# Attention gate columns computed by half products behind the heads, and applied from HBM

## The chip, the cores and the metric

One core of a Trainium2 chip runs the whole kernel. The metric is device time in microseconds; the kernel before takes 1495.14 us (median of 3 runs). TensorE (PE) multiplies, VectorE (DVE), ScalarE (ACT) and GpSimd (POOL) do the rest; transfers are issued from the queue of SyncE (SP), some from ACT's.

## The reference

```python
h = rms_norm(x, norm_w)                                  # x: 512 x 2048
(a_q, a_f, a_i, a_g, b_q, b_k, b_v, b_g, gate_a, gate_b) = split(h @ w_in)   # 8 x 1024, 2 x 2048 columns
ya = hgrn2_mixer(a_q, a_f, a_i, ...) * silu(a_g)
yb = diff_attention(b_q, b_k, b_v, ...) * silu(b_g)      # 8 heads of 128 columns
mixed = sigmoid(gate_a) * (ya @ w_branch_a) + sigmoid(gate_b) * (yb @ w_branch_b)
out = x + mixed @ w_out
```

The change concerns `b_g`, the 1024 gate columns of the attention, and `silu(b_g)`.

## The kernel before

All products are made from fp32r pieces: a factor is split into a rounded high part and a remainder, and a product of two factors is three matmuls (high-high, high-low, low-high). The stages follow each other on PE:

1. `proj_a` and `mix_a` (to about 465 us): the recurrent branch.
2. Eight attention heads. `proj_b(head)` (L445) projects `h` to 512 columns of the head: q, k, v and gate, 128 each. Its `gemm` (L164) walks 8 blocks of two K tiles; per block it loads 128x2x512 weights (L177), rounds them on ACT (L182), takes the remainder on DVE (L183), and issues 24 matmuls of 512 columns (L198), 192 in a head. `evac_rows` (L225) copies the four PSUM accumulators out on ACT (L228). Then q and k are normalised (L458 to L463) and the gate columns go through `silu` (L240).
3. `mix_b(head)` (L469) is the attention itself: eight transposes of q and k (L476), gains on ACT and DVE (L482, L483), six small copies between partition halves on ACT's DMA queue (L486 to L489), scores of four row blocks (L512, L513) through a minimum on DVE (L515) and an exponential on ACT (L518), the combination of the two softmaxes on DVE (L526), transposes of the weights (L534) and the values (L541). Block 0 to 2 are twelve score matmuls, block 3 is four. `finish` (L250) normalises the head's output, multiplies by the gate (L267), transposes it (L274, in `turn`, run later inside a following `gemm`), splits it and writes high and low part to `y_d` (L280).
4. Beside heads 3 to 6, `stage` (L718) prepares the half-sums of `h` for stage 6 (two of eight steps per head; each reads two 256 KB tiles of x and writes five to `hs_d`).
5. Four `gemm`s with `w_a`.
6. `halved` (L600): the two merge gates, 16 groups of 256 columns. A group is made by seven half products (a 2x2 scheme with seven multiplications instead of eight), each of 8 matmuls of 512 and 8 of 256 columns (L693). Per half product ACT rounds a quarter of the weights (L653), DVE takes the remainder (L654) and, for four, adds quarters (L645). `gate_dual` (L897) combines the results, applies the sigmoid (L899), in the first eight groups multiplies by `z_d` (L902), and writes `g_d`.
7. Four `gemm`s with `w_b` on `yb` read from `y_d`, and `halved` again for `w_out`.

The order on each engine is fixed when the program is built: a scheduler simulates a timeline and puts the instructions of different heads between each other, PE's matmuls of `mix_b(head)` among those of `proj_b(head + 1)`. At run time every engine keeps that order and waits where an operand isn't ready. Small tiles come from 49 slots handed out first in, first out (`Slots`, L48), so a new tile waits for the last reader of the tile that had its slot. PSUM has four accumulators for `gemm` and four `mix` tiles.

Of the kernel before, what the change touches and what calls it, by code (L numbers as in the profile page):

```python
# [17 lines left out]
P = 128  # L18
# [48 lines left out]
def hybrid_block(ctx: ExitStack, tc: tile.TileContext, xT, w_in, w_a, w_b, w_out,  # L67
# [96 lines left out]
    def gemm(wsrc, nk, a_hi, a_lo, stationary_w, evac, before=None, after=None, done=None, turn_at=1):  # L164
        accs = [acc_tile() for _ in range(4)]
        nb = nk // KC
        for kb in range(nb):
# [10 lines left out]
            with tc.high_priority(offset=PRIO):  # L178
                step = 1 if before is not None and kb == 0 else KC
                for c in range(0, KC, step):  # L180
                    cs = slice(c, c + step)
                    nc.scalar.activation(out=whi[:, cs, :], in_=raw[:, cs, :], func=AF.Copy)  # L182
                    nc.vector.tensor_tensor(out=wlo[:, cs, :], in0=raw[:, cs, :], in1=whi[:, cs, :].bitcast(F32),  # L183
                                            op=SUB)
# [3 lines left out]
            for j in range(4):  # L188
                for c in range(KC):
                    k = kb * KC + c  # L190
                    js = slice(j * P, (j + 1) * P)
                    if stationary_w:
                        prods = ((whi[:, c, js], a_hi[k]), (whi[:, c, js], a_lo[k]), (wlo[:, c, js], a_hi[k]))
                    else:
                        prods = ((a_hi[k][:, js], whi[:, c, :]), (a_hi[k][:, js], wlo[:, c, :]),
                                 (a_lo[k][:, js], whi[:, c, :]))
# [28 lines left out]
    def evac_rows(tiles):  # L225
        def evac(j, acc):
            s = slots.get()
            nc.scalar.activation(out=s[0], in_=acc, func=AF.Copy, scale=rstd_t[:, j:j + 1])  # L228
# [21 lines left out]
    def finish(o, gates, gain, rz, dest):  # L250
# [15 lines left out]
        for i in range(NT):  # L266
# [4 lines left out]
        def turn():  # L271
# [3 lines left out]
            slots.put(sq)  # L275
            yh, yl = slots.get(F32R), slots.get(F32R)
# [168 lines left out]
    def proj_b(head, done=None):  # L445
        tiles = []

        def src(raw, kb):
            rows = w_in[kb * KC * P:(kb + 1) * KC * P, 4 * WA:8 * WA].rearrange("(c p) (s n) -> p c s n", p=P, s=4)
            return [(raw[:, c, :].rearrange("p (s n) -> p s n", s=4), rows[:, c, :, head * P:(head + 1) * P])  # L450
                    for c in range(KC)]

        gemm(src, NK, h_hi, h_lo, False, evac_rows(tiles), turn_at=3 if head > 3 else 1, done=done)
# [12 lines left out]
        silu([s[0][:, 384:512] for s in tiles])  # L466
        return tiles

    def mix_b(head, tiles, bias, dest):  # L469
# [88 lines left out]
        finish(o, [t[0][:, 384:512] for t in tiles], gb, rz, dest)  # L558
# [181 lines left out]
    g_d = dram.tile([2, NK, P, T], F32, name="g_d")  # L740
    y_d = dram.tile([2, 2, NWA, P, T], F32, name="y_d")
# [104 lines left out]
    def freed_by(tiles, quarters, w, c0):  # L846
        def done(kb):
            raws2.extend((tiles[0][kb][1], tiles[1][kb][1]))
            if kb < 2:
                for name, half, c in (("11", 0, 0), ("12", 0, 1), ("22", 1, 1), ("21", 1, 0))[2 * kb:2 * kb + 2]:  # L850
                    quarters[name] = load_quarter(w, half, c0 + c * D // 2, raws2)
# [9 lines left out]
    for g in range(4):  # L861
# [6 lines left out]
        def along(kb):  # L868
# [10 lines left out]
            if g == 3:  # L879
                freed_by(ya, quarters, w_in, 8 * WA)(kb)  # L880
# [16 lines left out]
    def gate_dual(which, n):  # L897
        def gated(t, e):
            nc.scalar.activation(out=t[0], in_=t[0], func=AF.Sigmoid)  # L899
# [6 lines left out]
        def right(st):  # L906
            add_halves(st[2][0][:, rh], st[1][0])
            slots.put(st[1])
            gated(st[2], NS + n)
# [3 lines left out]
        def emit(p, acc, st):  # L913
# [11 lines left out]
            elif p == 3:  # L925
# [4 lines left out]
                if which == 0:  # L930
                    for e in (NS + n, n):
                        st_z[e] = t = slots.get()
                        nc.sync.dma_start(out=t[0], in_=z_d[e])
# [6 lines left out]
    items = []  # L940
# [168 lines left out]
```

## Time and profile before

| | us |
|---|---|
| runs | 1494.73, 1495.14, 1498.22 |
| profiled execution | 1496.41 |
| its span | 1494.3 |
| PE busy | 1483.4 |
| DVE, ACT, POOL busy | 1033.6, 720.9, 82.6 |

Spans and busy times are of the one profiled execution. A matmul's record is longer than its share of a stream of matmuls, since they overlap; what one costs in a stream is the distance from its start to the next start.

### The profile page before, as it was taken

The numbers are of one execution on the slowest core, as the hardware profiler recorded it, in microseconds if no ns is written. First come the engines' busy times: TensorE is split into PE (matmuls) and PEld (weight loads), VectorE is DVE, ScalarE is ACT, GpSimd is POOL, SyncE is SP. The second block draws the span as 40 slices with busy tenths as digits, with TensorE's granted clock in tenths as the row PEclk, the third lists the DMA queues.
The fourth block names the chain that finished last, engine by engine and source line by source line (L and its number), as shares of the span: only waits on it lengthen the run. The fifth ranks groups of instructions, "written<-read, shape, count | busy, mean of one in ns | idle before, by whom it ended". The sixth has DMA issues, their size and how long they took to land.

```text
span 1494.3 us, 21762 instructions
## 1 busy us (share of the span) xinstructions
PE 1483.4 (99%) x7956; PEld 1285.0 (86%) x7956; DVE 1033.6 (69%) x2005; ACT 720.9 (48%) x1092; POOL 82.6 (6%) x94
## 2 busy tenths in 40 slices
PE   9999999999999999999999999999999999999998
PEld 8888888888888888888888888888888888879998
DVE  7656666575585556666766555888888866798775
ACT  7632642544524545555555544555554544344332
POOL 1000000000001101101101100000000000000000
PEclk9999999999999999999999999999999999999999
DMA  7332322322323446465458787555444465575540
GB/s 250 99 99 80 103 86 85 109 75 85 113 72 121 118 128 198 125 185 168 149 169 275 245 274 242 154 168 155 142 135 141 130 216 191 189 226 157 154 119 32
DMA packets 270874, 222.83 MB, mean 149 GB/s; under 512 B 13040, under 2 KB 230768, under 8 KB 270768
## 3 DMA queue, kind: packets, MB, share of 16 engines
q1 hardware_dynamic: 266704, 214.88, 46.1%
q10 hardware_dynamic: 3984, 6.31, 1.6%
q8 instruction: 62, 1.02, 0.3%
q14 instruction: 44, 0.36, 0.1%
q0 software_dynamic: 80, 0.26, 0.1%
HBM read 179.46 MB, written 35.65 MB: 144 GB/s over the span
## 4 chain that ended last, share of the span: by engine, by line
PE 93%; DMA 3%; DVE 2%; ACT 1%; SPq 1%; issue 0%; DVEq 0%; ACTq 0%
PE acc L198 54%; PE acc L693 26%; PE mix L693 4%; PE mix L317 3%; PE mix L541 1%; DMA s<-in_xT_dram 1%; PE mix L512 1%; PE mix L513 1%; PE mix L534 1%; DMA hs_d<-s 1%; PE mix L402 0%; DMA b<-in_w_in_dram 0%; PE mix L274 0%; DVE s L578 0%; DMA b<-in_w_b_dram 0%; PE mix L476 0%
## 5 line engine op out<-in xcount | busy, mean ns | idle before, releaser
L198 PE MATMUL acc<-b,b 128*128 128x512 f32 x3840 | 912.0, 393 | 2.7 <-ACT b L182 2.6
L198 PEld LDWEIGHTS acc<-b,b 128*128 128x128 f32 x3840 | 713.2, 188 | 146.2 <-ACT b L182 3.2
L183 DVE TENSOR_TENSOR b<-b,b 128x1024 fp32r<-128x1024 f32 (+1 forms) x161 | 195.7, 1216 | 183.4 <-ACT b L182 168.8
L182 ACT ACTIVATE b<-b 128x1024 fp32r<-128x1024 f32 (+1 forms) x161 | 169.2, 1051 | 277.7 <-PE acc L198 218.0
L653 ACT ACTIVATE b<-b 128x1024 fp32r<-128x1024 f32 x168 | 178.0, 1061 | 249.1 <-PE acc L693 155.6
L693 PE MATMUL acc<-s,b 128*128 128x256 f32 (+1 forms) x1792 | 284.4, 314 | 2.1 <-ACT b L653 1.0
L693 PEld LDWEIGHTS acc<-s,b 128*128 128x128 f32 x1792 | 255.3, 191 | 24.9 <-ACT b L653 1.2
L654 DVE TENSOR_TENSOR b<-b,b 128x1024 fp32r<-128x1024 f32 x168 | 205.3, 1222 | 34.5 <-ACT b L653 33.7
L693 PE MATMUL acc<-b,b 128*128 128x256 f32 (+1 forms) x896 | 143.4, 314 | 0.0
L693 PEld LDWEIGHTS acc<-b,b 128*128 128x128 f32 x896 | 128.2, 191 | 10.8
L645 DVE TENSOR_TENSOR b<-b,b 128x1024 f32<-128x1024 f32 x96 | 117.3, 1222 | 1.1
L693 PE MATMUL mix<-s,b 128*128 128x256 f32 (+1 forms) x448 | 72.5, 314 | 1.8 <-DVE b L654 1.3
L693 PEld LDWEIGHTS mix<-s,b 128*128 128x128 f32 x448 | 64.3, 191 | 7.6 <-DVE b L654 1.5
L333 DVE COPY_PREDICATED s<-s,mix 128x128 f32<-128x128 uint8 (+3 forms) x176 | 52.0, 338 | 14.1 <-PE mix L317 13.0
L577 ACT ACTIVATE s<-s 128x256 fp32r<-128x256 f32 x96 | 37.1, 411 | 49.3 <-DVE s L974 23.0
L518 ACT ACTIVATE s<-s,mn 128x128 f32<-128x128 f32 (+3 forms) x64 | 35.5, 555 | 24.8 <-DVE mn L515 24.7
L317 PE MATMUL mix<-qm,s 128*128 128x192 f32 x256 | 46.8, 326 | 0.0
L317 PEld LDWEIGHTS mix<-qm,s 128*128 128x128 f32 x256 | 42.7, 190 | 1.6
L461 POOL TENSOR_TENSOR qr<-qs,mhalf 128x4 f32<-128x4 f32 x32 | 35.4, 1116 | 114.8 <-DVE qs L460 114.8
L578 DVE TENSOR_TENSOR s<-s,s 128x256 fp32r<-128x256 f32 x96 | 38.3, 421 | 3.8 <-ACT s L577 3.5
L515 DVE CUSTOM_DVE_ANT_0 s<-mix,bias 128x128 f32<-128x128 f32 (+3 forms) x64 | 28.9, 487 | 13.1 <-PE mix L513 12.8
L228 ACT ACTIVATE s<-acc,rstd_t 128x512 f32<-128x512 f32 x48 | 32.5, 678 | 10.5 <-PE mix L541 7.3
(159 smaller groups left out, 1091.8 us busy)
## 6 DMA issues: line engine op xcount, KB each, us to landing
b<-in_w_in_dram SPq DMA_DIRECT2D x240, 256.0 KB, 3.0
b<-in_w_in_dram SPq DMA_DIRECT2D x64, 512.0 KB, 4.1
b<-in_w_out_dram SPq DMA_DIRECT2D x32, 512.0 KB, 4.2
s<-in_xT_dram SPq DMA_DIRECT2D x46, 256.0 KB, 4.1
hs_d<-s SPq DMA_DIRECT2D x40, 256.0 KB, 3.8
y_d<-s SPq DMA_DIRECT2D x32, 256.0 KB, 2.8
b<-y_d SPq DMA_DIRECT2D x32, 256.0 KB, 4.4
b<-in_w_a_dram SPq DMA_DIRECT2D x32, 256.0 KB, 4.0
```

The lines of the kernel that those rows point to most:

```text
L182: nc.scalar.activation(out=whi[:, cs, :], in_=raw[:, cs, :], func=AF.Copy)
L183: nc.vector.tensor_tensor(out=wlo[:, cs, :], in0=raw[:, cs, :], in1=whi[:, cs, :].bitcast(F32), op=SUB)
L198: nc.tensor.matmul(accs[j], lhsT=l, rhs=r, start=(k == 0 and n == 0), stop=(k == nk - 1 and n == 2))
L317: nc.tensor.matmul(ps[:, i * 192:(i + 1) * 192], lhsT=kt[:, tt * P:(tt + 1) * P], rhs=qm[:, tt * 192:(tt + 1) * 192], start=True, stop=True)
L333: nc.vector.copy_predicated(out=ov[:, :, a:b], mask=kv[:, :, s0:s0 + b - a], data=dv[:, :, s0:s0 + b - a])
L518: nc.scalar.activation(out=pr[c][0][:, 0:n], in_=pr[c][0][:, 0:n], func=AF.Exp, scale=-1.0, bias=mn[:, e:e + 1], accum_out=z[:, e:e + 1])
L577: nc.scalar.activation(out=out[..., lh], in_=x, func=AF.Copy)
L578: tt(out=out[..., rh], in0=x, in1=out[..., lh].bitcast(F32), op=SUB)
L645: tt(out=r[x][0], in0=r[x][0], in1=r[y][0], op=ADD)
L653: nc.scalar.activation(out=xh[0], in_=x, func=AF.Copy)
L654: tt(out=xl[0], in0=x, in1=xh[0].bitcast(F32), op=SUB)
L693: nc.tensor.matmul(o, lhsT=l, rhs=r, start=(first and ks[0] == 0 and n == 0), stop=(ks[-1] == NS - 1 and n == len(prods) - 1), skip_group_ ...
```

## The change

`proj_b` projects to 384 columns instead of 512: the weights read, rounded and multiplied are q, k and v alone, and `silu` leaves the heads. `finish` of a head multiplies by the row factor alone, now on ACT instead of DVE, and writes the transposed, ungated output in one tile to `yf_d`. The gate columns become four more groups at the head of `halved` in stage 6 (16 to 20 groups); their `gate_dual` applies Silu, multiplies by the head's output read back from `yf_d`, splits the product and writes it to `y_d`. The eight steps of `stage` are handed to heads 2 to 7 as 1, 1, 2, 1, 1, 2 instead of two each to heads 3 to 6.

```diff
-    def gemm(wsrc, nk, a_hi, a_lo, stationary_w, evac, before=None, after=None, done=None, turn_at=1):
+    def gemm(wsrc, nk, a_hi, a_lo, stationary_w, evac, before=None, after=None, done=None, turn_at=1, width=T):
...
-                    nc.scalar.activation(out=whi[:, cs, :], in_=raw[:, cs, :], func=AF.Copy)
...
+                    ws = slice(0, width)
+                    nc.scalar.activation(out=whi[:, cs, ws], in_=raw[:, cs, ws], func=AF.Copy)
...
-                        nc.tensor.matmul(accs[j], lhsT=l, rhs=r, start=(k == 0 and n == 0),
+                        nc.tensor.matmul(accs[j][:, ws], lhsT=l, rhs=r, start=(k == 0 and n == 0),
...
-        for i in range(NT):
+        for i in range(NT) if gates is None else ():
+            nc.scalar.activation(out=y[:, i * P:(i + 1) * P], in_=o[:, i * P:(i + 1) * P], func=AF.Copy,
+                                 scale=rr[:, i:i + 1])
+        for i in range(NT) if gates is not None else ():
...
+            if gates is None:
+                y_t = slots.get()
+                nc.scalar.activation(out=y_t[0], in_=yt, func=AF.Copy, scale=gain)
+                nc.sync.dma_start(out=yf_d[dest[1]], in_=y_t[0])
+                slots.put(y_t)
+                return
...
-        gemm(src, NK, h_hi, h_lo, False, evac_rows(tiles), turn_at=3 if head > 3 else 1, done=done)
+        gemm(src, NK, h_hi, h_lo, False, evac_rows(tiles, 3 * P), turn_at=3 if head > 3 else 1, done=done,
+             width=3 * P)
...
-        silu([s[0][:, 384:512] for s in tiles])
...
-        finish(o, [t[0][:, 384:512] for t in tiles], gb, rz, dest)
+        finish(o, None, gb, rz, dest)
...
+    STAGE = {1: (0,), 2: (1,), 3: (2, 3), 4: (4,), 5: (5,), 6: (6, 7)}
...
-        staged = [(k, stage_in(k)) for k in (2 * head - 4, 2 * head - 3)] if 2 <= head < 6 else []
+        staged = [(k, stage_in(k)) for k in STAGE.get(head, ())]
...
+        other = n + (NWA // 2 if which == 2 else NS)
+
         def gated(t, e):
+            if which == 2:
+
+                nc.scalar.activation(out=t[0], in_=t[0], func=AF.Silu)
+                z = st_z[e]
+                tt(out=t[0], in0=t[0], in1=z[0], op=MUL)
+                zh, tl = z[0].bitcast(F32R), t[0].bitcast(F32R)
+                nc.scalar.activation(out=zh, in_=t[0], func=AF.Copy)
+                tt(out=tl, in0=t[0], in1=z[0], op=SUB)
+                nc.sync.dma_start(out=y_d[1, 0, e], in_=z[0])
+                nc.sync.dma_start(out=y_d[1, 1, e], in_=t[0])
+                slots.put(z, t)
+                return
...
-    items = []
+    items = [(w_in, 7 * WA + n * P, 7 * WA + T + n * P, three_slots, gate_dual(2, n)) for n in range(NWA // 2)]
```

The scheduler makes another order of all this. PE, the scores of head 3, before: they stand inside the product of head 4 (L198), which goes on behind them; 30 of its matmuls stand between the last score of blocks 0 to 2 (L513) and the first transpose of the weights (L534). `s` are slots, `acc` the accumulators.

```order
L512 MATMUL mix<-s_366_5497,s_362_5482 128x256
L513 MATMUL mix<-s_368_5499,s_362_5482 128x256
...
L534 MATMUL mix<-ident,s_369_5512 128x128
L534 MATMUL mix<-ident,s_371_5529 128x128 x2
L512 MATMUL mix<-s_365_5496,s_361_5481 128x512
```

PE, the same place now (L522, L523 are the scores, L544 the transposes, L199 the product):

```order
L199 MATMUL acc<-b_327_5875,b_16_125 128x384
L522 MATMUL mix<-s_346_5440,s_342_5425 128x256 x2
L523 MATMUL mix<-s_348_5442,s_342_5425 128x256 x2
...
L523 MATMUL mix<-s_349_5443,s_343_5426 128x384
L544 MATMUL mix<-ident,s_350_5456 128x128
L544 MATMUL mix<-ident,s_352_5473 128x128 x2
L522 MATMUL mix<-s_346_5440,s_342_5425 128x512
...
L523 MATMUL mix<-s_349_5443,s_343_5426 128x512
L199 MATMUL acc<-b_330_6141,b_1_110 128x384
```

The twelve scores, the transposes and the four scores of block 3 have moved to the border between the products of heads 4 and 5; the first L199 row above is the last matmul of head 4, the last row the first of head 5, and nothing of a product stands between. Head 5's scores stand in the same way at the border of heads 6 and 7; at the border of head 7 and the `w_a` product stand head 6's second transposes and block 3.

ACT at that border, before: the copies of the product out of PSUM (L228) stand behind the copies of transposed weights (L536).

```order
L518 ACTIVATE s_377_5573,z<-s_377_5573,mn 128x512
L518 ACTIVATE s_378_5574,z<-s_378_5574,mn 128x512
L182 ACTIVATE b_333_6285<-b_332_6284 128x1024
L577 ACTIVATE s_439_6175<-s_400_5697 128x256
L536 COPY s_379_5595<-mix 128x384
L228 ACTIVATE s_406_5950<-acc,rstd_t 128x512
```

ACT now (L528 exponentials, L587 staging, L229 the copies out of PSUM, L546 copies of transposed weights):

```order
L528 ACTIVATE s_354_5490,z<-s_354_5490,mn 128x384
L587 ACTIVATE s_373_5610<-s_379_5618 128x256
...
L587 ACTIVATE s_377_5614<-s_380_5619 128x256
L528 ACTIVATE s_351_5457,z<-s_351_5457,mn 128x128
L528 ACTIVATE s_353_5474,z<-s_353_5474,mn 128x256
L528 ACTIVATE s_355_5491,z<-s_355_5491,mn 128x384
L229 ACTIVATE s_384_5887<-acc,rstd_t 128x384
L546 COPY s_356_5510<-mix 128x128
```

The first copy out of PSUM of head 4's product now stands behind the exponentials of the second softmax of head 3's blocks 0 to 2, and its slot (number 17) is the one of a softmax tile, `s_353_5474`, which it may overwrite only when DVE has combined block 1.

## Rows read from the trace of the kernel before

**Rows 1.** Page, parts 1 and 2: busy time and share of each engine; granted clock.

```profile
PE 1483.4 (99%) x7956; PEld 1285.0 (86%) x7956; DVE 1033.6 (69%) x2005; ACT 720.9 (48%) x1092; POOL 82.6 (6%) x94
PEclk9999999999999999999999999999999999999999
```

**Rows 2.** Stretches: PE, PEld, DVE, ACT, POOL busy (instructions), clock, DMA share, GB/s.

```profile
700.00:750.00 50.00, 50.00 (x246) 42.01 (x245) 36.27 (x100) 29.72 (x60) 6.50 (x6) 1.00 0.55 168
1000.00:1050.00 50.00, 50.00 (x289) 44.01 (x288) 44.52 (x53) 25.73 (x34) 0.00 (x0) 1.00 0.55 167
1200.00:1250.00 50.00, 47.73 (x257) 41.17 (x257) 28.39 (x33) 20.40 (x26) 0.00 (x0) 1.00 0.68 212
1300.00:1350.00 50.00, 46.69 (x283) 41.19 (x282) 46.63 (x88) 21.86 (x37) 0.00 (x0) 1.00 0.70 221
```

**Rows 3.** Timeline of PE in head 2: start, us, line, operation, tiles, shape, count.

```profile
565.95 10.23 PE L198 MATMUL acc<-b,b 128*128 128x512 f32 x44
...
600.34 0.33 PE L512 MATMUL mix<-s,s 128*128 128x384 f32 x1
600.51 0.62 PE L198 MATMUL acc<-b,b 128*128 128x512 f32 x2
600.97 0.34 PE L513 MATMUL mix<-s,s 128*128 128x384 f32 x1
601.15 2.46 PE L198 MATMUL acc<-b,b 128*128 128x512 f32 x10
```

**Rows 4.** Timeline of PE in `halved`: groups of 16 matmuls, 8 of 512, 8 of 256 columns.

```profile
957.52 2.96 PE L693 MATMUL acc<-b,b 128*128 128x512 f32 x16
960.31 2.96 PE L693 MATMUL acc<-s,b 128*128 128x512 f32 x16
...
977.07 2.96 PE L693 MATMUL acc<-b,b 128*128 128x512 f32 x16
```

**Rows 5.** Timeline of PE around head 4's attention.

```profile
693.29 0.93 PE L476 MATMUL mix<-ident,s 128*128 128x128 f32 x7
693.98 8.91 PE L198 MATMUL acc<-b,b 128*128 128x512 f32 x38
...
709.10 0.28 PE L513 MATMUL mix<-s,s 128*128 128x256 f32 x1
709.22 7.45 PE L198 MATMUL acc<-b,b 128*128 128x512 f32 x32
716.50 0.49 PE L534 MATMUL mix<-ident,s 128*128 128x128 f32 x3
...
717.75 0.63 PE L198 MATMUL acc<-b,b 128*128 128x512 f32 x2
```

**Rows 6.** Timeline of ACT in the same stretch (ACTq is its queue).

```profile
694.39 0.67 ACT L482 ACTIVATE s<-mix,gq 64x512 fp32r<-64x512 f32 x1
...
700.16 0.47 ACTq L489 DMA_DIRECT2D s<-s  x1
...
705.37 0.60 ACT L518 ACTIVATE s<-s,mn 128x384 f32<-128x384 f32 x1
```

**Rows 7.** Timeline of DVE there: the combination of blocks 0, 1 and 2.

```profile
711.52 1.27 DVE L526 SCALAR_TENSOR_TENSOR s<-s,f,s 128x128 f32<-128x128 f32 x3
```

**Rows 8.** Line L489, all heads: from issue of the copy to its landing.

```profile
DMA to landing us min/median/max: 2.3/4.5/6.5
```

**Rows 9.** Groups of instructions by line: count | busy us, mean ns | idle before.

```profile
L182 ACT ACTIVATE b<-b 128x1024 fp32r<-128x1024 f32 x159 | 168.0, 1056 | 277.2 <-PE acc L198 218.0 <-issue 21.5 <-DMA b<-in_w_in_dram 7.9
L183 DVE TENSOR_TENSOR b<-b,b 128x1024 fp32r<-128x1024 f32 x159 | 194.4, 1223 | 183.0 <-ACT b L182 168.4 <-PE acc L198 12.1 <-DMA b<-in_w_in_dram 1.2
L902 DVE TENSOR_TENSOR s<-s,s 128x512 f32<-128x512 f32 x16 | 11.0, 688 | 0.5 <-ACT s L899 0.5
```

**Rows 10.** Timeline of PE at the start, and its longest pause later.

```profile
1.04 6.30 PE L109 MATMUL mix<-ones 128*128 128x128 f32 x28 [1.04 <-DVE mhalf L103]
...
1233.70 1.66 PE L198 MATMUL acc<-b,b 128*128 128x512 f32 x6 [2.27 <-ACT b L182]
```

More of the change, by code (lines that the diff above doesn't have):

```diff
@@ L181, in gemm @@
                     cs = slice(c, c + step)
-                    nc.scalar.activation(out=whi[:, cs, :], in_=raw[:, cs, :], func=AF.Copy)
-                    nc.vector.tensor_tensor(out=wlo[:, cs, :], in0=raw[:, cs, :], in1=whi[:, cs, :].bitcast(F32),
-                                            op=SUB)
+                    ws = slice(0, width)
+                    nc.scalar.activation(out=whi[:, cs, ws], in_=raw[:, cs, ws], func=AF.Copy)
+                    nc.vector.tensor_tensor(out=wlo[:, cs, ws], in0=raw[:, cs, ws],
+                                            in1=whi[:, cs, ws].bitcast(F32), op=SUB)
             if after is not None and kb == nb - 1:
@@ L222, in two_cols, with evac_rows @@
         return src
-    def evac_rows(tiles):
+    def evac_rows(tiles, width=T):
         def evac(j, acc):
             s = slots.get()
-            nc.scalar.activation(out=s[0], in_=acc, func=AF.Copy, scale=rstd_t[:, j:j + 1])
+            nc.scalar.activation(out=s[0][:, 0:width], in_=acc[:, 0:width], func=AF.Copy, scale=rstd_t[:, j:j + 1])
             tiles.append(s)
@@ L448, in src @@
         def src(raw, kb):
-            rows = w_in[kb * KC * P:(kb + 1) * KC * P, 4 * WA:8 * WA].rearrange("(c p) (s n) -> p c s n", p=P, s=4)
-            return [(raw[:, c, :].rearrange("p (s n) -> p s n", s=4), rows[:, c, :, head * P:(head + 1) * P])
+            rows = w_in[kb * KC * P:(kb + 1) * KC * P, 4 * WA:7 * WA].rearrange("(c p) (s n) -> p c s n", p=P, s=3)
+            return [(raw[:, c, 0:3 * P].rearrange("p (s n) -> p s n", s=3), rows[:, c, :, head * P:(head + 1) * P])
                     for c in range(KC)]
-        gemm(src, NK, h_hi, h_lo, False, evac_rows(tiles), turn_at=3 if head > 3 else 1, done=done)
+        gemm(src, NK, h_hi, h_lo, False, evac_rows(tiles, 3 * P), turn_at=3 if head > 3 else 1, done=done,
+             width=3 * P)
         for s in tiles:
@@ L740, in hybrid_block @@
     g_d = dram.tile([2, NK, P, T], F32, name="g_d")
+    yf_d = dram.tile([NWA, P, T], F32, name="yf_d")
     y_d = dram.tile([2, 2, NWA, P, T], F32, name="y_d")
@@ L844, in hybrid_block, with freed_by @@
     vs, raws2 = [], deque()
-    def freed_by(tiles, quarters, w, c0):
+    def freed_by(tiles, quarters, w, c0, right=D // 2):
         def done(kb):
@@ L850, in done @@
                 for name, half, c in (("11", 0, 0), ("12", 0, 1), ("22", 1, 1), ("21", 1, 0))[2 * kb:2 * kb + 2]:
-                    quarters[name] = load_quarter(w, half, c0 + c * D // 2, raws2)
+                    quarters[name] = load_quarter(w, half, c0 + c * right, raws2)
         return done
@@ L879, in along @@
             if g == 3:
-                freed_by(ya, quarters, w_in, 8 * WA)(kb)
+                freed_by(ya, quarters, w_in, 7 * WA, T)(kb)
         gemm(two_cols(w_a, g * H, D // 2 + g * H), NWA, each(ya[0]), each(ya[1]), True, keep_z, done=along,
@@ L908, in right @@
             slots.put(st[1])
-            gated(st[2], NS + n)
+            gated(st[2], other)
         st_z, seen = {}, set()
@@ L929, in emit @@
                     right(st)
-                if which == 0:
-                    for e in (NS + n, n):
+                if which != 1:
+                    for e in (other, n):
                         st_z[e] = t = slots.get()
-                        nc.sync.dma_start(out=t[0], in_=z_d[e])
+                        nc.sync.dma_start(out=t[0], in_=z_d[e] if which == 0 else yf_d[e])
             else:
```

4 lines of the change are left out of this document (2 added, 2 removed).

## The prediction

> **What bounds the kernel now.** I read the busy shares first: PE has 1483.4 of 1494.3 us, and the clock is at its upper level throughout [rows 1]. Then the stretches [rows 2]: beside the heads (700 to 750) and the half products (1000 to 1050) PE is busy for all 50 us, while DVE has 36.3 and 44.5 us, ACT 29.7 and 25.7. The only breaks stand at the change to `w_b` (47.73 of 50) and the start of `w_out` (46.69); the change touches neither. So the time is the sum of PE's matmuls, as long as each finds its operands when PE comes to it. What a matmul costs in that sum is its distance to the next start. A change pays if it shortens that sum without making PE wait, and both have to be worked out.
>
> **The matmuls.** Removed: 8 heads x 192 = 1536 matmuls shrink from 512 to 384 columns. A run of 44 of 512 columns took 10.23 us [rows 3]; the last stretches 0.39 us past its start (L512, L513 and L198 single records), so (10.23 - 0.39)/43 = 0.229 us each; the runs of 38 and 32 in head 4 give 0.230 and 0.228 [rows 5]. I take 0.228. A matmul of 384 columns occurs in the scores: from L512 at 600.34 to the next start at 600.51 are 0.17 us, from L513 at 600.97 to 601.15 are 0.18 [rows 3]. I take 0.1745, between them. Saved: 1536 x 0.0535 = 82 us; with 0.230 and 0.17 it is 92, with 0.228 and 0.18 it is 74, but the records are rounded to 0.01 us and 256 columns cost 0.12 us (below), so that 384 half way between 0.12 and 0.228 is 0.174: the ends worth keeping are 79 and 85.
>
> Added: four groups of seven half products of 16 matmuls. Such sixteens start every 2.79 us (960.31 to 977.07 is six of them, 16.76 us, [rows 4]); a group is 7 x 2.793 = 19.55 us, four are 78.2. The arithmetic of seven instead of eight products would have saved more, but each half product is made of more and shorter matmuls: 8 of 512 take 8 x 0.228 = 1.82 us, so the 8 of 256 take 0.97, 0.12 each, more than half of 0.228. PE's sum: -82 + 78 = **-4 us**, between -7 and -1.
>
> The Trainium skill (TensorE: Matmul & The Clock Gate, "Back-to-back issue gap") puts a warm matmul of N columns at N/2.4 + 2.5 ns. By that page 1536 x 53.3 ns = 82 us go and 4 x 56 x (215.8 + 109.2) ns = 73 us come, so its sum would be -9 us. The rows disagree on the fixed part (0.12 us for 256 columns), and the measurement decides.
>
> **What hides the rest.** ACT and DVE lose more than they gain in the heads: 64 rounding and 64 remainder passes shrink by a quarter (DVE 1.22 us each, [rows 9], so about 0.3 us x 8 = 2.4 us a head), the silu goes. They were not the bound there, so this is worth nothing by itself. In the new groups DVE does two more subtractions than in the first merge groups (L902's kind, 0.69 us, [rows 9]): 44.5 us in 50 [rows 2] is 17.4 in 19.55; with 1.4 more it is 18.8, 96%. The rounding runs some half products ahead, so I take 0; if DVE needed all the idle time that it has now (2.15 us a group), it costs 1.4 x 4 = 5.5 us. The 8 writes and 8 reads of `yf_d` and the 16 writes of `y_d` go through SP among loads; DMA is at 0.55 in the gate stretch [rows 2] and the `w_b` product that needs `y_d` comes sixteen groups later: 0. Staging: two steps move from heads 3 to 6 into heads 2 and 7 (per step two reads and five writes of 256 KB on SP, ahead of the following weight loads). With two steps a head PE never paused in 700 to 750 [rows 2]: 0, and up to 2 us at head 7, where `ya` is loaded too.
>
> **The new wait.** A head's product now takes 192 x 0.1745 = 33.5 us instead of 43.8, but the attention that runs beside it is a chain with the same length. In the order above this shows at the border of heads 4 and 5: all sixteen scores of head 3 and the transposes that need their softmax stand back to back, with no matmul of a product between them. Behind them in PE's queue is the whole product of head 5, and it couldn't pass anyway: its accumulator is freed by L229, which waits for DVE's combination of block 1. Everything after waits with it. What PE pays there, in us after head 3's last transpose of q and k (L486):
>
> - PE has 36 matmuls of head 4 left: 36 x 0.1745 = 6.3.
> - The second softmax needs the third pair of copies to the other partition half. In head 4 of the kernel before the last transpose ended at 693.29 + 0.93 = 694.22 and the last copy (L489) was issued at 700.16, 5.9 later [rows 5, 6]. Now a rounding stands ahead of that copy on ACT and waits for head 4's last matmuls: 6.3 and three quarters of 1.06 [rows 9], 7.1.
> - Landing: 4.5 (2.3 to 6.5, [rows 8]), so 11.6.
> - Six matmuls with the low part of k, 0.5; minimum, exponential and combination up to block 1: in head 4 from the last L513 at 709.10 to the end of the second combination, about 712.3, 3.2 [rows 5, 7]; now the exponentials of three blocks (0.60 for 384 columns, [rows 6]) and four staging copies stand ahead, up to 4.1. I take 3.6: 15.7.
> - Transposes of blocks 0 and 1 and the scores of block 3: 716.50 to 717.75 = 1.25 [rows 5]. Head 5 starts at 17.0.
>
> Of these 17.0 PE worked 6.3 + 1.7 (twelve scores, 8 x 0.12 + 4 x 0.175) + 1.25 = 9.25. The pause is 7.7 us; with the short ends (5.9, 2.3, 3.2) it is 4.0, with the long ones (7.1, 6.5, 4.1) 10.2. The other end of the pause would be none if something of a product stood between, and nothing does. At the border of heads 6 and 7 the same order stands behind 38 matmuls (6.6 us), with three more staging copies ahead of the copy: 3.7 to 11.3, middle 7.5. I take 7 for each, below the middle, since with PE and the DMA queues idle the copies land sooner. At the border of head 7 and `w_a` the softmax has been given 33 + 6 matmuls (6.8 us) against 3.2 to 4.1 needed; the first `w_a` matmul waits for one L229 behind a rounding and a staging copy: about 0.6 us (0 to 2). At the other borders the products start with no score run ahead: 0.
>
> **Sum.** -4 + 7 + 7 + 0.6 = +10.6 us on a span of 1494.3, so about 1505; the profiled execution (1496.41) is 1.3 us over the median 1495.14, so against the median 1495.1 + 10.6 = 1505.7, rounded to **1506**.
>
> **Rivals.**
> - *The borders cost nothing* (not slower): the softmax chain is done when PE gets there, because ACT and DVE have less to do in a head. Then -4: 1491. For it: PE has not paused in any head, whatever the order. Against it: in head 4 the chain from the last transpose to the combination of block 1 took 712.3 - 694.2 = 18 us [rows 5, 7], and now it has 6.3 + 1.7. It decides if that chain can be done in 8 us; two pauses below 2 us each would do.
> - *The clock falls in the pauses.* Rows show no pause over 2.27 us between matmuls [rows 10], and there the clock stayed up [rows 1]. At the start 28 matmuls of 128 columns took 6.30 us, 0.22 each, against (0.93 - 0.27)/6 = 0.11 in head 4 [rows 5, 10]: half the pace, the lower level, after PE had done nothing. If PE comes back at that pace for as long (6 us) after each of the two pauses, it loses 3 us each time: 1506 + 6 = 1512. The Trainium skill (TensorE: Matmul & The Clock Gate, Part 1) says that the gate halves the clock after idle time, which speaks against making PE wait here. The scores within the pause, a few matmuls, speak against the fall.
> - *DVE bounds the new groups*: 1506 + 5.5 = 1511.
>
> **Chances.** Pauses as worked out, total 3 to 18 us above the PE sum: 0.65. No pauses: 0.17. Clock falls as well: 0.12. DVE bounds the groups: 0.06. About 0.3% (4.5 us) is what a measurement of this kernel can tell from no change. Faster by more (below 1490.7) is a little over half of the second case: 0.10. Within it: the rest of that case, 0.07, and the pauses at their short ends (-4 + 8 = +4), 0.13: 0.20. Slower: 0.70. The range leaves out the no-pause cases below 1494 and the worst sums: 1494 (two pauses of 1.5 us) to 1515 (two of 11 us, or clock and middle pauses).
>
> **What would show it.** In the trace of the changed kernel: starts of L199 in the heads 0.174 us apart and sixteens of L703 2.79 us apart (PE's sum); pauses of PE ahead of L523 and L544 at the borders of heads 4 and 5 and of 6 and 7, ended by the copy's landing (L499) and by DVE's combination (L536), with no others in the heads; PE near 100% in the four new groups; the clock at 1.00 around the pauses. The prediction is wrong if those borders are closed up, if PE pauses in the new groups behind DVE, or if pauses stand where I have put none, at head 7 behind SP's queue above all.

## The result, and the profile after

The changed kernel takes 1510.99 us (median; 1510.54 to 1512.74) against 1495.65 for the kernel before on the same chip: ratio 1.0104, 95% interval 1.0092 to 1.0115, so 15.5 us or 1.0% slower. The forecast was 1506 within 1494 to 1515. The profiled execution took 1512.74 us with a span of 1511.0, 16.7 more than the span before; it is the slowest of the four, so the losses read from its trace are 1 to 2 us larger than those of the medians.

The page after, busy time and granted clock (parts 1 and 2), which answer to [rows 1]:

```profile
PE 1486.0 (98%) x8404; PEld 1337.0 (88%) x8404; DVE 1068.3 (71%) x2021; ACT 727.4 (48%) x1135; POOL 84.3 (6%) x94
PEclk9999999999999999899999999999999999999999
```

PE's busy time hardly moved, as the sum of the matmuls said, though it holds matmuls at the lower clock: slice 17 of the clock (604 to 642 us) is an 8 where [rows 1] has only nines. The stretches, with the columns of [rows 2]:

```profile
550.00:600.00 50.00, 50.00 (x309) 49.65 (x308) 28.94 (x83) 27.32 (x63) 6.92 (x6) 1.00 0.49 153
600.00:650.00 50.00, 45.12 (x260) 43.65 (x259) 32.02 (x92) 27.20 (x64) 7.90 (x7) 0.90 0.42 132
700.00:750.00 50.00, 44.12 (x258) 42.43 (x257) 32.46 (x96) 28.03 (x65) 6.77 (x6) 0.93 0.71 216
750.00:800.00 50.00, 46.85 (x234) 39.31 (x233) 25.27 (x77) 23.18 (x48) 7.59 (x6) 1.00 0.75 245
800.00:850.00 50.00, 48.40 (x233) 40.19 (x232) 21.85 (x70) 22.02 (x43) 1.01 (x1) 1.00 0.83 274
860.85:939.03 78.18, 78.18 (x449) 68.83 (x448) 70.58 (x82) 45.39 (x59) 0.00 (x0) 1.00 0.59 185
```

PE is full in the first heads and in the four new groups (the last row). It idles 4.9 and 5.9 us in the two stretches that hold the borders of heads 4/5 and 6/7, there with a mean clock of 0.90 and 0.93, and 3.2 and 1.6 us around head 7 and in `w_a`.

How long each stage lasted, from its first matmul to that of the next, in the profiled execution of every kernel of this study (us; "heads, w_a" is the sum of the three columns before it):

| kernel | heads 0-3 | heads 4-7 | w_a | heads, w_a | merge gates | w_b to the end |
|---|---|---|---|---|---|---|
| before | 209.0 | 203.6 | 97.7 | 510.3 | 312.5 | 260.6 |
| after | 164.0 | 185.2 | 101.2 | 450.4 | 389.4 | 260.7 |
| e1, staging back | 167.1 | 178.7 | 99.6 | 445.4 | 389.7 | 260.5 |
| e2, heads only | 168.5 | 190.1 | 102.2 | 460.8 | 311.9 | 260.6 |
| e3, groups only | 211.0 | 210.3 | 95.1 | 516.4 | 389.5 | 260.7 |
| e4, turn late | 168.4 | 164.3 | 96.8 | 429.5 | 389.4 | 260.5 |
| e5, before with turn late | 210.2 | 207.3 | 95.1 | 512.6 | 311.1 | 260.4 |
| e6, own slots | 164.4 | 159.6 | 128.8 | 452.8 | 389.3 | 260.5 |
| e7, pauses filled | 164.1 | 192.4 | 98.9 | 455.4 | 389.7 | 261.2 |
| e9, turn late, staging back | 165.9 | 165.9 | 97.2 | 429.0 | 389.9 | 260.8 |
| e10, before, new staging | 210.7 | 203.2 | 95.9 | 509.8 | 311.3 | 260.8 |
| e11, half the filling | 164.1 | 181.4 | 99.9 | 445.4 | 389.5 | 260.4 |

The groups cost 389.4 - 312.5 = 76.9 us in every kernel that has them. Heads and `w_a` gave back 59.9 us where the matmuls alone are worth 81. The missing 21 us are the loss.

**The pauses.** PE after, at the border of heads 4 and 5 (the place of [rows 5]; L278 is the turn, L486 the transposes of q and k, L522 and L523 the scores, L544 the transposes of the weights, L199 the product):

```profile
606.72 0.27 PE L278 MATMUL mix<-ident,s 128*128 128x128 f32 x1
606.83 0.27 PE L486 MATMUL mix<-ident,s 128*128 128x128 f32 x1
...
607.38 0.82 PE L486 MATMUL mix<-ident,s 128*128 128x128 f32 x6
607.95 6.50 PE L199 MATMUL acc<-b,b 128*128 128x384 f32 x36
614.28 0.40 PE L522 MATMUL mix<-s,s 128*128 128x256 f32 x2
...
614.93 0.33 PE L523 MATMUL mix<-s,s 128*128 128x384 f32 x1
617.17 0.83 PE L522 MATMUL mix<-s,s 128*128 128x256 f32 x3 [1.91 <-ACT s L587]
617.80 0.95 PE L523 MATMUL mix<-s,s 128*128 128x256 f32 x3
621.72 1.15 PE L544 MATMUL mix<-ident,s 128*128 128x128 f32 x3 [2.96 <-DVE s L536]
...
623.51 0.63 PE L522 MATMUL mix<-s,s 128*128 128x512 f32 x1
623.94 0.63 PE L523 MATMUL mix<-s,s 128*128 128x512 f32 x1
624.37 4.31 PE L199 MATMUL acc<-b,b 128*128 128x384 f32 x15
```

Two idle stretches, 1.91 and 2.96 us, ahead of the second softmax's scores and of the transposes. The first is put down to L587, a staging step that the scores do not read. What the first of them (L522) read last is the low part of q, in a copy (L496) that ACT's queue issued at 613.67. It landed 3.3 us later, at 616.9, and the scores start 0.25 us after that:

```profile
613.67 0.47 ACTq L496 DMA_DIRECT2D s<-s  x1
...
622.15 0.58 ACT L229 ACTIVATE s<-acc,rstd_t 128x384 f32<-128x384 f32 x1 [1.96 <-DVE s L536]
```

```profile
DMA to landing us min/median/max: 3.3/3.3/3.3
```

The row of L229 is the closed border itself: L229, which frees head 4's accumulator, waits for DVE's combination (L536) because of the slot that it shares with a softmax tile. The chain of waits followed back through the same stretch (start, us, engine, tile, line):

```profile
607.10 0.22 PE mix L278 x2
607.58 0.69 ACT s L282
608.26 0.58 ACT s L492
...
610.68 0.85 ACT b L183
611.55 0.81 DVE b L184
612.43 0.42 DVE s L594
612.88 1.44 DVE s L493 x2
...
618.26 0.29 DVE s L525
...
619.44 1.34 DVE s L588 x4
...
621.40 0.27 DVE s L536
```

Shown from the turn of head 2's output on, it goes through the transposed q and k, and on its way passes a rounding (L183), a remainder (L184) and staging (L594, L588) that stand ahead of it on ACT and DVE. Ahead of the turn this view has only the product (40 matmuls of L199, 6.94 us): PE came to the turn when its place in the queue was reached. At the border of heads 6 and 7 the same happens:

```profile
708.18 0.65 PE L522 MATMUL mix<-s,s 128*128 128x256 f32 x3 [2.98 <-DVE rz L532]
...
711.72 1.21 PE L544 MATMUL mix<-ident,s 128*128 128x128 f32 x3 [2.48 <-DVE s L536]
...
714.43 3.87 PE L199 MATMUL acc<-b,b 128*128 128x384 f32 x16
```

**The clock.** Behind these pauses matmuls run at half pace: the scores of 512 columns start 0.43 us apart (623.51, 623.94 and the next start at 624.37, at the end of the first of these timelines), where matmuls of that size in [rows 3] start 0.23 apart. The granted clock had fallen behind the first pause already, with the second still to come (PE alone):

```profile
615.00:617.20 2.20, 0.29 (x3) 1.00 0.59 191
617.50:619.00 1.50, 1.25 (x6) 0.50 0.64 181
```

At the border of heads 6 and 7 it fell within the second pause (1.00 from 708.2 to 709.5 us, 0.50 from 709.7). A mean of 0.90 and 0.93 over 50 us, between the levels 1.0 (2.4 GHz) and 0.5 (1.2 GHz), is 10 and 7 us at the lower level. Some 3 and 2 us of that are idle anyway, so 7 + 5 = 12 us of matmuls ran at half pace and cost 6 us. The Trainium skill (TensorE: Matmul & The Clock Gate, Part 1) says that the clock falls to half after idle time and comes back with activity; the trace agrees, for pauses of 1.9 to 3.0 us with six scores between two of them.

The loss adds up: idle 4.9 + 5.9 + 3.2 + 1.6 = 15.5, half pace 6, together 21.5 of 21.

### The profile page after: what moved, and what is told of

It reads as the page before. It is cut to its first block, busy times and chain, and to the rows that moved or that the text cites. A ratio compares the mean times of both kernels' runs of the same rounds, so it can differ in the third digit from the quotient of the medians.

```text
span 1511.0 us, 22888 instructions
## 1 busy us (share of the span) xinstructions
PE 1486.0 (98%) x8404; PEld 1337.0 (88%) x8404; DVE 1068.3 (71%) x2021; ACT 727.4 (48%) x1135; POOL 84.3 (6%) x94
## 3 DMA queue, kind: packets, MB, share of 16 engines
q1 hardware_dynamic: 269264, 219.07, 46.5%
## 4 chain that ended last, share of the span: by engine, by line
PE 92%; DMA 4%; DVE 3%; ACT 1%; issue 0%; SPq 0%; ACTq 0%; DVEq 0%
PE acc L199 48%; PE acc L703 31%; PE mix L703 5%; PE mix L327 3%; PE mix L551 1%; DMA yf_d<-s 1%; PE mix L544 1%; PE mix L522 1%; DMA b<-hs_d 1%; PE mix L523 1%; PE mix L412 0%; PE mix L278 0%; DVE s L588 0%; DVE b L184 0%; PE mix L109 0%
## 5 line engine op out<-in xcount | busy, mean ns | idle before, releaser
L199 PE MATMUL acc<-b,b 128*128 128x512 f32 (+1 forms) x3840 | 827.7, 371 | 2.0 <-ACT b L183 1.0
L199 PEld LDWEIGHTS acc<-b,b 128*128 128x128 f32 x3840 | 697.3, 189 | 91.4 <-ACT b L183 1.6
L663 ACT ACTIVATE b<-b 128x1024 fp32r<-128x1024 f32 x196 | 207.7, 1061 | 281.3 <-PE acc L703 176.1
L703 PE MATMUL acc<-s,b 128*128 128x256 f32 (+1 forms) x2048 | 331.1, 317 | 2.1 <-ACT b L663 1.0
L703 PEld LDWEIGHTS acc<-s,b 128*128 128x128 f32 x2048 | 295.5, 190 | 30.3 <-ACT b L663 1.2
L184 DVE TENSOR_TENSOR b<-b,b 128x1024 fp32r<-128x1024 f32 (+2 forms) x161 | 178.6, 1110 | 179.4 <-ACT b L183 164.5
L183 ACT ACTIVATE b<-b 128x1024 fp32r<-128x1024 f32 (+2 forms) x161 | 155.7, 967 | 249.8 <-PE acc L199 193.9
L664 DVE TENSOR_TENSOR b<-b,b 128x1024 fp32r<-128x1024 f32 x196 | 239.1, 1220 | 34.7 <-ACT b L663 32.2
L703 PE MATMUL acc<-b,b 128*128 128x256 f32 (+1 forms) x1024 | 167.0, 317 | 0.0
L587 ACT ACTIVATE s<-s 128x256 fp32r<-128x256 f32 x96 | 37.0, 411 | 46.8 <-DVE s L1000 23.0
L528 ACT ACTIVATE s<-s,mn 128x128 f32<-128x128 f32 (+3 forms) x64 | 35.4, 554 | 15.5 <-DVE mn L525 15.4
L588 DVE TENSOR_TENSOR s<-s,s 128x256 fp32r<-128x256 f32 x96 | 38.9, 427 | 5.3 <-ACT s L587 5.1
L229 ACT ACTIVATE s<-acc,rstd_t 128x384 f32<-128x384 f32 (+1 forms) x48 | 29.1, 610 | 11.5 <-PE mix L551 5.1
L943 ACT COPY s<-acc 128x512 f32<-128x512 f32 x60 | 34.1, 568 | 0.1
```

The costliest lines, as they stand in the source:

```text
L183: nc.scalar.activation(out=whi[:, cs, ws], in_=raw[:, cs, ws], func=AF.Copy)
L184: nc.vector.tensor_tensor(out=wlo[:, cs, ws], in0=raw[:, cs, ws], in1=whi[:, cs, ws].bitcast(F32), op=SUB)
L199: nc.tensor.matmul(accs[j][:, ws], lhsT=l, rhs=r, start=(k == 0 and n == 0), stop=(k == nk - 1 and n == 2))
L587: nc.scalar.activation(out=out[..., lh], in_=x, func=AF.Copy)
L588: tt(out=out[..., rh], in0=x, in1=out[..., lh].bitcast(F32), op=SUB)
L663: nc.scalar.activation(out=xh[0], in_=x, func=AF.Copy)
```

## The experiments

The theory at this point: the attention is a chain, the shortened product no longer covers it, and where the order closes a head's border, PE waits. The rivals: the new staging map makes the waits; what else changed in the heads or the groups does; the clock or the shared slots decide.

**e1, the staging map of the kernel before.**

```diff
-    STAGE = {1: (0,), 2: (1,), 3: (2, 3), 4: (4,), 5: (5,), 6: (6, 7)}
+    STAGE = {2: (0, 1), 3: (2, 3), 4: (4, 5), 5: (6, 7)}
```

> The changed kernel with the eight staging steps handed out as in the kernel before (two each to heads 2 to 5 of the list, none late). My theory (the shorter product no longer covers the attention chain of the head before, so pauses stand at the borders of heads 4/5 and 6/7, and the clock falls after them): staging is a passenger, the time stays at 1511 give or take 4 us, with one or two pauses of 2 us or more ahead of scores or transposes at head borders, perhaps at other borders than before. Rival (the new staging map makes the waits, by its copies on ACT ahead of the exponentials and its transfers beside head 7): 1500 or less, no pause at 615 to 622 and 705 to 712 us, and no waits at head 7 and in w_a.

Measured: 1505.68 us, ratio 1.0068 (1.0051 to 1.0085). Heads 4 to 7 still lose, in other places: the longest distances between two matmul starts there are 2.7 us at 658, 2.1 at 669, 1.6 at 705 and 1.4 at 747 us, and the clock is at its lower level for some 10 us in all. So the pauses do not come from the staging map, but 5 of the 21 us hang on where it puts them. Neither bound of the expectation was met; the map is a small part, not nothing.

**e2, the heads' part alone:** the four groups and the gating are left out (of three edits, the one that drops the groups).

```diff
-    items = [(w_in, 7 * WA + n * P, 7 * WA + T + n * P, three_slots, gate_dual(2, n)) for n in range(NWA // 2)]
+    items = []
```

> The heads' part alone: heads of 384 columns, and no gate groups at all (the attention output goes ungated into y_d, so this leaves out the gate columns' product and the gating; its time is read for the heads and w_a only, and for what the groups add). My theory: of the 82 us that 1536 shorter matmuls save only about 60 arrive, because of the pauses and the lower clock: 1495 - 82 + 22 = 1435, between 1431 and 1440, with w_a ending near 861 us and the same pauses. Rival (the groups' additional reads and rounding made the waits in the heads, or the groups cost more than 78): pauses gone, 1413 to 1418.

Measured, in one run: 1445.2 us. The pauses are there without any group, so the groups' traffic does not make them. They are larger than expected, 460.8 - 429.5 = 31 us against e4, since the scheduler's new order makes PE wait in more places: beside 3.0 us at 623 and 3.8 at 710 us between two starts, there are 2.2 us in head 2, at 525, and four of 1.2 to 2.0 in head 7, at 757 to 764. The loss is no fixed sum; it depends on the order.

**e3, the groups' part alone:** heads of 512 columns, the gate columns computed and not used.

```diff
-            rows = w_in[kb * KC * P:(kb + 1) * KC * P, 4 * WA:7 * WA].rearrange("(c p) (s n) -> p c s n", p=P, s=3)
+            rows = w_in[kb * KC * P:(kb + 1) * KC * P, 4 * WA:8 * WA].rearrange("(c p) (s n) -> p c s n", p=P, s=4)
...
-        gemm(src, NK, h_hi, h_lo, False, evac_rows(tiles, 3 * P), turn_at=3 if head > 3 else 1, done=done,
-             width=3 * P)
+        gemm(src, NK, h_hi, h_lo, False, evac_rows(tiles), turn_at=3 if head > 3 else 1, done=done)
```

> The groups' part alone: the four new groups stand in the merge stage, but the heads still compute 512 columns (the gate columns are computed and not used, extra work against both kernels). My theory: the product of a head is long enough again, no pause in any head, clock at its upper level throughout, and the time is 1495 + 78 = 1573, between 1571 and 1576. Rival (pauses come from what else changed in the heads, the ungated finish on ACT and the new staging map, not from the shorter product): pauses of 2 us or more at the borders stay, 1580 or more. Rival 2 (DVE bounds the new groups): the four groups take more than 79 us in the gate stage.

Measured, in one run: 1578.91 us, of which the gates are 389.5. Heads 1 to 6 run at 51 us each without a pause, with the ungated `finish` and the new staging in place: the length of the product is what closes or opens the borders. What stands above the 1573 expected is in head 7 (57.2 us):

```profile
797.61 0.41 PE L521 MATMUL mix<-s,s 128*128 128x384 f32 x1 [1.19 <-DMA s<-s]
...
802.23 0.69 PE L522 MATMUL mix<-s,s 128*128 128x384 f32 x1 [2.36 <-DMA s<-s]
```

Scores of head 6 wait for their copies. The changed kernel has such waits in `w_a` at the same time of the run (0.62 and 1.60 us at 797 and 803 us, for `s<-s` too).

**e10, the new staging map alone in the kernel before,** to see whether it makes these waits.

```diff
-        staged = [(k, stage_in(k)) for k in (2 * head - 4, 2 * head - 3)] if 2 <= head < 6 else []
+        staged = [(k, stage_in(k)) for k in {1: (0,), 2: (1,), 3: (2, 3), 4: (4,), 5: (5,), 6: (6, 7)}.get(head, ())]
```

> The kernel before with nothing changed but the hand-out of the staging steps (heads 2 to 7 instead of 3 to 6, two steps beside head 7). e3_groups_only had pauses of 1.6 and 2.8 us and 3.4 us of low clock within the w_a product though its heads were of full length. My theory now (the late staging steps cost what e3_groups_only and e1_staging_back differ by from their neighbours): 1500 to 1502, with pauses ahead of head 7's scores in w_a. Rival (those pauses need the gate groups' early loads or the ungated output's write): 1495 give or take 2.

Measured: 1494.74 us, ratio 0.9995 (0.9986 to 1.0004). No change and no pause in heads or `w_a`: my theory for this one fell. What makes the 4 to 6 us at head 7 and `w_a` in the changed kernel and in e3, and not here, in e4 or in e9, is not settled. The copies in question took 4.7 to 7.1 us to land in those two kernels, the copies of the same stretch 3.8 to 5.1 here and 4.7 to 5.9 in the kernel before, so slow landing alone does not tell the kernels apart.

**e4, the turn late.** The transposes of q and k of head h go into the same four `mix` tiles as the output of head h - 1, and in the changed kernel they stand right behind its turn, in every head (L278 and L486 interleave at 606.72 and 606.83 above). This takes the turn behind them:

```diff
-        gemm(src, NK, h_hi, h_lo, False, evac_rows(tiles, 3 * P), turn_at=3 if head > 3 else 1, done=done,
+        gemm(src, NK, h_hi, h_lo, False, evac_rows(tiles, 3 * P), turn_at=None if head else 1, done=done,
...
             lows.append(lo)
+        while later:
+            later.pop(0)()
```

> The changed kernel with one thing moved: the transposes of the previous head's output (the turn) are issued behind this head's transposes of q and k instead of inside its product, so that the transposes of q and k no longer wait, through the four mix tiles in PSUM, for the previous head's output. My theory (the chain from the transposes of q and k to the combination sets the borders, so that starting it earlier in the head takes the pauses away): pauses at the borders gone or under 1 us, clock at its upper level throughout, the heads save about 80 us, 1491 to 1499. Rival (the length of the product alone decides, whatever starts the chain): pauses of 5 us or more in sum stay, 1505 to 1512.

Measured: 1491.92 us, ratio 0.9977 (0.9968 to 0.9986): 19 us faster than the changed kernel, and faster than the kernel before. PE in e4 at head 4, whose product starts at 578.87 (L553 the values, L486 and L278 as above, L524 the scores):

```profile
580.42 1.05 PE L553 MATMUL mix<-s,s 128*128 128x128 f32 x8
581.31 0.38 PE L486 MATMUL mix<-ident,s 128*128 128x128 f32 x2
...
589.57 0.38 PE L278 MATMUL mix<-ident,s 128*128 128x128 f32 x2
...
595.07 0.28 PE L524 MATMUL mix<-s,s 128*128 128x256 f32 x1
...
602.10 5.03 PE L199 MATMUL acc<-b,b 128*128 128x384 f32 x28
```

The transposes start 2.4 us into the product, ahead of the turn, and the scores end in the middle of it. The same stretches as above, in e4:

```profile
600.00:650.00 50.00, 50.00 (x307) 49.49 (x306) 34.69 (x105) 28.48 (x66) 7.25 (x6) 1.00 0.54 164
700.00:750.00 50.00, 49.20 (x298) 47.38 (x297) 33.96 (x99) 28.80 (x65) 11.20 (x8) 1.00 0.86 281
```

No border pause, and the clock at 1.00. What the move shows is that the attention is a **loop**: transposes of q and k, copies, softmaxes, values, turn, and only then the next head's transposes. How far into the next head's product the transposes of q and k start (first L486, or L476 before, less the first matmul of the next product, us):

| head | 0 | 1 | 2 | 3 | 4 | 5 | 6 | 7 |
|---|---|---|---|---|---|---|---|---|
| before | 4 | 6 | 6 | 17 | 21 | 20 | 18 | 22 |
| after | 4 | 20 | 29 | 32 | 23 | 31 | 18 | 25 |
| e4 | 4 | 4 | 5 | 2 | 3 | 3 | 3 | 5 |
| e6 | 7 | 16 | 22 | 27 | 36 | 42 | 52 | 58 |

From head 0's to head 7's transposes the changed kernel needs 784.9 - 461.7 = 323 us, 46 a round, while an undisturbed head takes 39 to 40. So the attention slips back, by 28 us from head 0 to head 3, until at heads 3 and 5 it reaches the end of the product and PE has to wait; the wait lets it catch up. Before, a head took 51 us and a round fitted.

The 46 us are a mean, and they belong to the order that the scheduler built: in heads 0 to 3 PE is never idle, so what comes late there comes late by its place in PE's queue. ACT had finished head 2's output at 603.97, and PE turned to it at 606.72:

```profile
602.83 1.14 ACT L268 ACTIVATE s<-mix,rr 128x128 f32<-128x128 f32 x4 [1.25 <-DVE rr L265]
```

How short a round could be in another order, with the turn left in front, no run shows.

**e5, the same move in the kernel before.**

```diff
-        gemm(src, NK, h_hi, h_lo, False, evac_rows(tiles), turn_at=3 if head > 3 else 1, done=done)
+        gemm(src, NK, h_hi, h_lo, False, evac_rows(tiles), turn_at=None if head else 1, done=done)
...
             lows.append(lo)
+        while later:
+            later.pop(0)()
```

> Control: the kernel before with the same move of the turn as in e4_turn_late (the previous head's output transposed behind this head's transposes of q and k). My theory (the move helps because the shortened product no longer covers the chain; before, PE had no pause in any head): no change, 1495 give or take 2 us. Rival (the move is worth something by itself, and would have been in the kernel before): 1493 or less.

Measured: 1496.57 us, ratio 1.001 (1.000 to 1.002). The move is worth nothing where the product covers the loop. (Its trace has one wait of 1.7 us, ahead of scores at 799 us, of the kind left open under e10.)

**e9, both:** e4 with e1's staging map.

```diff
-    STAGE = {1: (0,), 2: (1,), 3: (2, 3), 4: (4,), 5: (5,), 6: (6, 7)}
+    STAGE = {2: (0, 1), 3: (2, 3), 4: (4, 5), 5: (6, 7)}
```

> e4_turn_late with the staging steps handed out as in the kernel before: both remedies together. My theory: what is left in e4_turn_late at head 7 and in w_a is about 2 us (1.1 us ahead of a score, 0.9 in w_a), so 1489.5 to 1491.5. Rival (two steps a head in the now shorter heads bring back a pause): 1493 or more.

Measured: 1491.72 us, ratio 0.9972 (0.9960 to 0.9983), no different from e4. Two steps a head are hidden in the shorter heads too, once the loop is cut.

**e6, own slots for the copies out of PSUM,** the other half of the closed border. The eight slots are taken from the 49, so all else shares 41.

```diff
-            s = slots.get()
+            s = slots.get(ring=ring)
...
+    own = deque(slots.free.popleft() for _ in range(8))
...
-        slots.put(*tiles)
+        own.extend(i for _, i in tiles)
```

> The changed kernel with eight slots kept for the copies of the projection out of PSUM, so that these copies (L229 of the changed kernel) no longer wait for a softmax tile of the head before; the transposes still wait for the turn as in the changed kernel. My theory says that the pause is the attention chain meeting a closed border: with the border open, TensorE goes on with the next head's product and the pauses at the borders 4/5 and 6/7 go, worth 11 to 13 us and the 6.6 us of the low clock: 1493 to 1499, unless the order makes a new closed stretch in w_a, where two runs of twelve scores now stand with little between (then up to 1503). Rival (only an earlier start of the chain helps, as in e4_turn_late, and the shared slots are no cause): pauses of 2 us or more at head borders remain, 1505 or more.

Measured: 1514.32 us, ratio 1.0116 (1.0101 to 1.0131). The borders opened as expected, and heads 4 to 7 are the shortest of all (159.6 us, clock 1.00). But the loop still takes 46.8 us a round (44.7 to 49.3, with PE never idle in a head), so nothing stops the attention from slipping: head 7's transposes come 58 us late, and heads 6 and 7 are left for `w_a`, which takes 128.8 us instead of 97:

```profile
764.01 1.08 PE L544 MATMUL mix<-ident,s 128*128 128x128 f32 x3 [2.81 <-DVE s L536]
...
791.89 1.04 PE L486 MATMUL mix<-ident,s 128*128 128x128 f32 x8
...
797.87 0.74 PE L522 MATMUL mix<-s,s 128*128 128x256 f32 x3 [4.61 <-DMA s<-s]
```

My number (1493 to 1503) failed, and so did the rival's reason: the pauses at the borders were caused by the shared slots, yet to take them away only moved the debt to the end. Of the two, the loop makes the loss (e4 and e9 are without it), the slots set its place.

**e7 and e11, the pauses filled with matmuls,** to price the clock (extra work, unused).

```diff
-                e = 2 * i + c
+                e = 2 * i + c; [nc.tensor.matmul(ps[:, 384:512], lhsT=kl2[c][0][:, ts].bitcast(F32), rhs=ident, start=True, stop=True) for _ in range((16, 24)[c] if i == 2 and head in (3, 5) else 0)]
```

> The changed kernel with matmuls of 128 columns into unused PSUM columns put into the two border pauses, 16 behind block 2's first scores and 24 behind its second, in the heads 3 and 5 alone (extra work, its output unused). The pauses keep their length, but TensorE works in them. My theory (the granted clock falls to its lower level because TensorE does nothing in the pauses, and costs about 3 us after each): clock 1.00 from 600 to 730 us, matmuls of 384 columns 0.174 us apart behind the pauses, 1505 give or take 2. Rival (the pauses of 2 to 3.5 us are too short to matter and the slow records have another cause): the lower level stays at both places, 1511 or more.

Measured: 1518.95 us, ratio 1.0155 (1.0139 to 1.0171). The clock stayed up at both places, as the stretches show, but the filling was too long, and the heads with it:

```profile
600.00:650.00 50.00, 49.07 (x328) 48.51 (x327) 31.19 (x89) 25.82 (x60) 8.13 (x7) 1.00 0.41 125
700.00:750.00 50.00, 49.68 (x331) 48.67 (x329) 29.45 (x81) 26.16 (x58) 7.70 (x6) 1.00 0.67 204
```

With 8 and 12 instead of 16 and 24:

> e7_pauses_filled with half the filling, 8 and 12 matmuls. In e7_pauses_filled the clock stayed at 1.00 through both places, but a float matmul of 128 columns was two passes of 0.11 us, so that the filling took 3.5 and 5.4 us and was longer than the pauses of 2.1 to 3.3 and 2.8 to 3.5 us. With half of it, 1.7 and 2.6 us, the filling fits inside. My theory: clock 1.00 from 600 to 740 us, head 4 at about 46.5 us instead of 49.9 and head 6 at about 46 instead of 49.3, 1504 to 1507 in all. Rival (the low clock costs nothing of its own, the time behind the pauses is lost to something else): head 4 and head 6 as long as in the changed kernel, 1511.

Measured: 1508.69 us (1507.27 to 1513.92), ratio 1.0092 (1.0071 to 1.0114); the profiled execution has a span of 1505.4 and a clock of 1.000. PE at the border of heads 4 and 5:

```profile
614.82 1.95 PE L524 MATMUL mix<-ident,s 128*128 128x128 f32 x16
617.01 0.65 PE L522 MATMUL mix<-s,s 128*128 128x256 f32 x3 [0.24 <-DMA s<-s]
...
618.03 2.84 PE L524 MATMUL mix<-ident,s 128*128 128x128 f32 x24
622.27 0.81 PE L544 MATMUL mix<-ident,s 128*128 128x128 f32 x3 [1.40 <-DVE s L536]
...
623.85 3.31 PE L199 MATMUL acc<-b,b 128*128 128x384 f32 x18
```

The chain sets the pause, and it took 0.8 us longer here, at least in part for the filling itself: it writes into the mix tile of block 2's scores, and DVE's minimum of that block waited 0.59 us for its last matmul:

```profile
620.90 0.56 DVE L525 CUSTOM_DVE_ANT_0 s<-mix,bias 128x384 f32<-128x384 f32 x1 [0.59 <-PE mix L524]
```

So head 4 is 49.65 us long, against 49.88, and not the 46.5 that I expected; head 6 is 47.7 against 49.3. But from the transposes to head 5's first matmul there are 1.58 us (622.27 to 623.85) instead of 2.65 (621.72 to 624.37): matmuls at full pace return a microsecond, and as much in the product behind (head 5 39.7 against 40.8). In the traces heads and `w_a` are 5.0 us shorter than in the changed kernel, of which 2 us are waits around head 7 that fell otherwise; in the medians it is 2 us (the traced execution is the fastest of its four, that of the changed kernel the slowest), and the intervals of the two ratios overlap. In the trace the clock's return is thus worth some 3 us where the rows at half pace give 6, with the filling's own delay against it; the times do not resolve it.

## Why the prediction was right, point by point

**The matmuls (-82 and +78, -4 in all): right.** The 81 us and the 76.9 us stand in the table; the second holds 1.3 us that the pause ahead of `w_b` became shorter, so the groups are 78.2. In e4, which is the change without its pauses, the kernel is 4.0 us faster by its median (2.1 to 4.8 by the interval), as the sum of PE's matmuls said. The Trainium skill's gap for warm matmuls (TensorE: Matmul & The Clock Gate, "Back-to-back issue gap") would have made it -9; the measurement is outside that.

**What hides the rest: right for the groups.** PE is full in the four groups with DVE at 70.58 of 78.18 us, 17.6 a group instead of the 18.8 of the text. The rival that DVE bounds them did not happen. The staging steps cost nothing by themselves (e10, e9).

**The pauses: right in place and mechanism, too long by 1.5 to 2 us each.** They stand at the two borders forecast and at no other border between two heads, ahead of the scores and of the transposes, ended by a copy and by DVE's combination, with L229 held as the text says. From the last transpose of q and k (608.20) the terms came out so: 36 matmuls 6.3 us (6.3 forecast); the second softmax's scores after 9.0 (11.6); from the last of them, at 618.2, to the transposes 3.5 (3.6); head 5 after 16.2 (17.0). The term mis-sized is the way to those scores. The forecast let them wait for the last copy (L499 now), behind a rounding on ACT; but that one carries the low part of k, which only the later scores (L523) read. The first (L522) wait for the copy of L496, issued after 5.5 us where 7.1 were entered, ahead of that rounding, and landed 3.3 later instead of 4.5 (4.3 at the border of heads 6 and 7). Against this, the matmuls at half pace took longer than forecast: the second softmax's scores 1.1 us instead of 0.5, transposes and block 3 2.65 instead of 1.25. Idle came to 4.9 and 5.5 us where 7 and 7 were entered.

**The clock: the likeliest case left it out, and that was wrong.** It was a rival with a chance of 0.12 and 3 us for each pause. The text held the scores within the pause against a fall; the clock fell even so, to 0.50 for 10 and 7 us. By the rows at half pace 6 us went there, of which e11 returned about half; its filling held DVE back in the same stretch, so the rest is not settled.

**Head 7 and `w_a`: missed.** 0.6 us were entered and 5.1 us of idle time stand there, among them 1.8 ahead of head 6's values at 759, 0.7 ahead of a `w_a` matmul that waits for L229, and 2.2 ahead of scores at 797 and 803. The step that failed is that behind that border nothing was entered: the attention of heads 6 and 7 arrives as late there as elsewhere, and its scores wait for copies inside `w_a`. Why those copies are late is not settled (e10).

So the likeliest sum, +10.6, met +16.7 with three misses: the pauses 3.6 us shorter than entered, head 7 and `w_a` 4.5 longer, the clock 6. That the sum came out 5 us off in the medians is in part luck, since the first miss hid most of the second; the range held because the rivals' prices were in it.

**What the text did not see** is why the chain stood at the border at all. It read the closed borders from the order and priced two. The cause is the loop through the turn, of which a round takes 46 us in the built order. The rows of before do not show that length: there the transposes of q and k stand 4 to 6 us into the next product up to head 2 and 17 to 22 from head 3 on, a step and no slip from head to head (what sets it no run shows). What could have been read is the order of the changed kernel, where they stand right behind the turn in every head; it would have pointed to e4's move.

## What to carry to other kernels

When a stream that hides a chain is made shorter, compare the chain's round trip, from one use of a shared buffer to the next, with the new length of the stream, not only the busy times of the engines: here DVE was busy for 71% and ACT for 48%, and the loop, in the order built, was still 7 us longer than a head. Take a dependency out of such a loop (what is transposed first, which buffer is shared) before you widen a border; a wait that is only unblocked comes back where the work ends. A change whose own sum is right may still be worth keeping: with the turn behind the transposes it is 0.2% faster than the kernel before, without it 1% slower.

## What the runs showed that I had not expected

- One pause of 1.9 us went ahead of a fall of the clock to its lower level (1.2 GHz), 0.3 us after PE had started again, and it stayed there for 10 us, over six scores and the second pause. The pause of 2.27 us in [rows 10] left it up (1.00 from 1230 to 1240 us).
- A matmul of 128 columns in float32 cost 0.22 us in a run of its own (16 of them from 615.07 to 618.56 us in e7, listed as x32), where transposes of the same size start 0.11 us apart. The filling of e7 was twice as long as meant for that reason.
- The scheduler's order reacts to small edits: e1 and e2 made PE wait in other places than the changed kernel, so that a loss in one order is no measure of the same edit in another.
